# Up-projections of a two-block transformer in fp32r: the three 256-column products of a weight tile become one 512-column and one 256-column product, wide ones first

## The chip, the cores and the metric

One NeuronCore of a Trainium2 chip runs the whole program. The time is the device time of one execution in microseconds; a lower time is better. Three executions of the kernel before took 1694.68 to 1696.04 us, median 1695.74 us.

## The reference

A sequence of 256 tokens with 1024 features passes through two blocks, in float32. The first has attention, an MLP, a state-space mixer and a second MLP; the second has, twice over, a SwiGLU, a convolution-plus-differential-attention mixer and another SwiGLU. The change is in the MLPs and the SwiGLUs:

```python
def squared_relu_mlp(x, w1, w2):                 # x (256, 1024), w1 (1024, 4096), w2 (4096, 1024), 2 layers
    return jnp.square(jax.nn.relu(x @ w1)) @ w2

def swiglu(h, w_gate, w_up, w_down):             # h (256, 1024), gate and up (1024, 2816), down (2816, 1024), 4 of them
    return (jax.nn.silu(h @ w_gate) * (h @ w_up)) @ w_down
```

## The kernel before

**Precision.** A float32 operand is split into a high part (cast to fp32r) and a low part (the remainder): `xh`, `xl` for the activations, `wh`, `wl` for the weights, `hh`, `hl` for the hidden values. A product is made of three on TensorE: high by high, high by low and low by high, summed in PSUM.

**Stages.** Ten stages follow each other: attn, mlp, ssm, mlp, ffn1, diff, ffn2, ffn1, diff, ffn2 (`STAGES`, L1783). `xh` and `xl` hold the stage's input transposed, 128 partitions by 8 blocks `k` of 128 features by 256 tokens.

**A dense stage** (`dense`, L994; `mlp`, L1015; `swiglu`, L1037) takes the first 512 hidden columns with `first`, then chunks of 256 columns with `later`: 14 chunks in each of the 2 MLPs ((4096 - 512) / 256) and 9 in each of the 4 SwiGLUs ((2816 - 512) / 256), so 28 and 36 chunks. A chunk makes one up-projection (MLP) or two (SwiGLU: gate, then up), applies the activation, splits the hidden values and, one chunk later (`LAG`, L624), adds its down-projection into four PSUM banks `acc`: 24 products of 512 columns.

**An up-projection** (`up_T`, L808) loads one 1 MB weight tile `st`, casts it to `wh` on ScalarE (2 pieces) and subtracts to `wl` on VectorE (2 pieces; `unit`, L727). For each of two column blocks `j` and eight `k` it makes three products of 256 columns into one PSUM bank `upT`; weights are stationary, activations move:

```python
mm(ps[:, j], wh[:, c], self.xh[:, k], start=k == 0, stop=False)
mm(ps[:, j], wh[:, c], self.xl[:, k], start=False, stop=False)
mm(ps[:, j], wl[:, c], self.xh[:, k], start=False, stop=k == KM - 1)
```

PSUM has 8 banks, of which `acc` holds four during a dense stage. ScalarE's Relu or Silu and a VectorE multiplication read `upT` directly; `split` (L913) makes `hh` (ScalarE) and `hl` (VectorE).

**Order.** All instructions are recorded first and ordered by a list scheduler (`schedule`, L328): on each engine the ready operation with the lowest `prio` (its place in the program plus `BIAS`, L628) goes next, by a cost table (`cost`, L150). The attn, ssm and diff stages use `up`, `up_T` and others, and pass through the same scheduler.

Of the kernel before, what the change touches and what calls it, by code (L numbers as in the profile page):

```python
# [10 lines left out]
F32 = mybir.dt.float32  # L11
F32R = mybir.dt.float32r
AF = mybir.ActivationFunctionType
ALU = mybir.AluOpType
# [113 lines left out]

class Op:
    __slots__ = ("seq", "eng", "call", "args", "kw", "cost", "prio", "preds", "succs", "allocs", "tiles", "table",  # L130
                 "start", "end", "est", "nbytes", "phase", "key")


ENG_OF = {"tensor": "PE", "scalar": "ACT", "vector": "DVE", "gpsimd": "POOL", "sync": "SP"}
# [7 lines left out]
def free(v):  # L142
    return int(np.prod(v.shape[1:]))
# [72 lines left out]
class Recorder:  # L216
# [42 lines left out]
    def record(self, eng, method, args, kw):  # L259
        o = Op()  # L260
        o.seq, o.eng, o.args, o.kw = len(self.ops), ENG_OF[eng], args, kw
        o.call = (eng, method)
        o.table = 0
        if method == "activation":
            f = kw.get("func", args[2] if len(args) > 2 else None)
            o.table = TABLES.get(f, 0)
        if method == "dma_start":
            out, writes, reads = kw["out"], [kw["out"]], [kw["in_"]]
        else:
            out = args[0] if args else kw["out"]  # L270
            writes = [out] + ([kw["accum_out"]] if "accum_out" in kw else [])
            reads = list(args[1:]) + [v for k, v in kw.items() if k not in OUTS]
        o.key = (self.where, getattr(getattr(out, "tile", None), "name", ""), o.eng)
        o.prio = o.seq + self.bias + BIAS.get(o.key, 0)
        writes = [v for v in writes if isinstance(v, View)]
        reads = [v for v in reads if isinstance(v, View)]
        if method == "dma_start":
            big = out if isinstance(out, View) else kw["in_"]
            o.nbytes = 4 * (big.p[1] - big.p[0]) * free(big)
            o.cost = 0.06 if o.eng == "SP" else 1.0  # L280
        else:
            o.nbytes = 0
            o.cost = cost(o.eng, method, args, kw, out, reads)
        o.preds, o.succs, o.allocs, o.tiles = {}, [], [], []
        if self.ahead is not None and self.ops:
            o.preds[self.ops[max(0, min(o.seq - 1, o.seq - self.ahead))]] = 0
        o.phase = None
        for v in reads:
            self.access(o, v, False)
        for v in writes:  # L290
            self.access(o, v, True)
        self.ops.append(o)
        return o
# [34 lines left out]
    def schedule(self):  # L328
# [21 lines left out]
        ready = {e: [] for e in engs}  # L350
        clock = {e: 0.0 for e in engs}
        table = [0]
        dma = [0.0]
        hwdge = [0.0]
        pe = PEClock()
# [74 lines left out]
        while done < total:  # L430
            best = None
            for e in engs:
                r = ready[e]
                if not r:
                    continue
                t0 = clock[e]
                if best is not None and t0 >= best[0]:
                    continue
                cand = [(est_of(o) if o.allocs else o.est, o) for o in r]
                m = min(x for x, _ in cand)  # L440
                t = max(t0, m)
                if t >= INF or (best is not None and t >= best[0]):
                    continue
                c = None
                for x, o in cand:
                    if x <= t + 1e-9:
                        k = o.prio
                        if e == "ACT" and o.table and o.table != table[0]:
                            k += SWITCH
                        if c is None or k < c[0]:  # L450
                            c = (k, o)
                k, o = c
                w = t + o.cost * HOLD
                h = None
                for x, q in cand:
                    if t < x < w and q.prio < o.prio - HOLD_MARGIN:
                        if h is None or q.prio < h[1].prio:
                            h = (x, q)
                if h is not None:
                    t, o = h  # L460
                    if best is not None and t >= best[0]:
                        continue
                best = (t, e, o)
            if best is None:
                self.stuck(npred)
            t, e, o = best
            ready[e].remove(o)
            take(o)
            o.start = t
            c = o.cost  # L470
            if e == "ACT" and o.table and o.table != table[0]:
                c += 1.283
                table[0] = o.table
            end = t + c
            if e == "PE":
                end = pe.run(t, c, columns(o))
            clock[e] = end
            if o.nbytes:
                if e == "SP":
                    hwdge[0] = max(hwdge[0], t + 0.55) + DMA_FIXED  # L480
                    dma[0] = max(dma[0], hwdge[0] + 0.65)
                else:
                    dma[0] = max(dma[0], t + 1.0)
                dma[0] += max(o.nbytes / 2.0 ** 20 * DMA_US, 0.05)
                end = dma[0] + DMA_END
            o.end = end
            order.append(o)
            done += 1
            for t_ in o.tiles:
                left[t_] -= 1  # L490
                last_end[t_] = max(last_end.get(t_, 0.0), end)
                p = t_.pool
                if p.phase >= 0:
                    phase_left[p.phase] -= 1
                    phase_end[p.phase] = max(phase_end[p.phase], end)
                    if phase_left[p.phase] == 0:
                        for q in waiting_phase.pop(p.phase, []):
                            push(q)
                if left[t_] == 0:
                    key = (p, t_.tag)  # L500
                    tagfree[key].append((last_end[t_] + 0.2, t_.slot))
                    held[key].remove(t_)
                    version[key] += 1
            for q in o.succs:
                lat = SAME[e] if q.eng == e else LAT.get((e, q.eng), 0.2)
                if o.nbytes:
                    lat = 0.2
                if q.preds[o]:
                    q.est = max(q.est, end + lat)
                else:  # L510
                    q.est = max(q.est, o.start)
                npred[q] -= 1
                if npred[q] == 0:
                    push(q)
# [34 lines left out]
FP32_MIN = 0.213  # L549
HOLD_MARGIN = 150  # L550
SWITCH = 500
DMA_US = 2.91
DMA_FIXED = 0.5
DMA_END = 0.7
# [2 lines left out]
T = 256  # L557
DM = 1024
KM = DM // 128
# [112 lines left out]
class Net:  # L672
    def __init__(self, tc, ctx, I, out):
# [14 lines left out]
        nc = self.nc  # L688
# [4 lines left out]
        self.neghalf = self.const.tile([128, 16], F32, name="neghalf")  # L693
        nc.gpsimd.memset(self.neghalf, -0.5)
        self.X = self.xp.tile([128, 2, DM], F32, name="X")
        self.xh = self.xp.tile([128, KM, T], F32R, name="xh")
        self.xl = self.xp.tile([128, KM, T], F32R, name="xl")

    def shaped(self, v, shape):

# [107 lines left out]
    def up_T(self, W, col, exact=False):  # L808

        ws = self.unit256(W, col, exact)  # L810
        ps = self.bank([128, 2, T], "upT")
        mm = self.nc.tensor.matmul
        for j in range(2):
            c = slice(j * 128, (j + 1) * 128)
            for k, (wh, wl) in enumerate(ws):
                if exact:
                    mm(ps[:, j], wh[:, c], self.x32[k // 4][:, k % 4], start=k == 0, stop=k == KM - 1)
                    continue
                mm(ps[:, j], wh[:, c], self.xh[:, k], start=k == 0, stop=False)
                mm(ps[:, j], wh[:, c], self.xl[:, k], start=False, stop=False)  # L820
                mm(ps[:, j], wl[:, c], self.xh[:, k], start=False, stop=k == KM - 1)
        return ps

    def bank(self, shape, name):
        return self.psum.tile(shape, F32, tag="ps", name=name)
# [189 lines left out]
    def mlp(self, W1, W2, finish_of):  # L1015
        nc = self.nc
# [8 lines left out]
                self.split_hid(hs, s, t)  # L1025

        def later(tp, c0, h):
            ps = self.up_T(W1, c0)
            r = tp.tile([128, 2, T], F32, tag="r", name="r")
            s = tp.tile([128, 2, T], F32, tag="s", name="s")  # L1030
            nc.scalar.activation(r, ps, AF.Relu)
            nc.vector.tensor_tensor(s, r, ps, op=ALU.mult)
            self.split(h, s)

        self.dense("mlp", DFF, first, later, W2, finish_of)
# [1 line left out]
    def swiglu(self, Wg, Wu, Wd, finish_of):  # L1037
# [11 lines left out]
                self.split_hid(hs, sg[t], t)  # L1049

        def later(tp, c0, h):
            pg = self.up_T(Wg, c0)
            s = tp.tile([128, 2, T], F32, tag="s", bufs=4, name="sg")
            nc.scalar.activation(s, pg, AF.Silu)
            pu = self.up_T(Wu, c0)
            nc.vector.tensor_tensor(s, s, pu, op=ALU.mult)
            self.split(h, s)

        self.dense("ffn", DFF2, first, later, Wd, finish_of)
# [760 lines left out]
```

## Time and profile before

| what | value |
|---|---|
| median of three executions | 1695.74 us (1694.68 to 1696.04) |
| the profiled execution's own time | 1694.3 us |
| its span, first to last instruction | 1692.4 us |
| PE (TensorE products) busy | 1676.7 us, 99% |
| DVE (VectorE) busy | 1123.6 us, 66% |
| ACT (ScalarE) busy | 878.0 us, 52% |
| weight transfers (1 MB each) | 267, landing after 4.8 us (median) |

The profile counts PE as busy from the start of a product to its modelled end, and products overlap in the pipeline: what one product costs in a stream is the distance from its start to the next one's start, not its duration. Names: `upT` is the PSUM bank of an up-projection in a chunk, `acc` a bank of the down-projection, `up` a 512-column projection elsewhere, `tr` a transpose, `wh`/`wl` the split weights, `st` the landed tile, `X` the residual stream. All instructions carry line L539, the place where the scheduler issues them, so the names tell them apart.

### The profile page before, as it was taken

The page shows a single profiled execution, that of the slowest core. Times are in us where ns is not written, and L with a number is a line of the kernel's source. Part 1 is how long each engine was busy: PE and PEld are TensorE (multiplying, and loading weights), DVE is VectorE, ACT ScalarE, POOL GpSimd, SP SyncE. Part 2 cuts the span into 40 slices and gives each one's busy share as a digit, 9 for nine tenths or more (in the row PEclk, how much of TensorE's full clock was granted, in tenths as well). Part 3 has the DMA queues.
Part 4 walks back from the last instruction along what each step waited for, and adds up shares of the span by engine and source line. Part 5 has one row for each costly group of instructions (what it writes and reads, how often), then busy time and mean ns, then how long its engine had stood idle before and what let it go on. Part 6 is the DMA issues. An engine that isn't in the chain of part 4 may idle for free.

```text
span 1692.4 us, 25721 instructions
## 1 busy us (share of the span) xinstructions
PE 1676.7 (99%) x10454; PEld 1476.2 (87%) x10454; DVE 1123.6 (66%) x1702; ACT 878.0 (52%) x1524; POOL 47.2 (3%) x50
## 2 busy tenths in 40 slices
PE   9999999999999999999999999999999999999999
PEld 8888998899988999889998658999899998579998
DVE  7766555899999555585545987554555458976541
ACT  5644444589995444454444366444454343565440
POOL 0000000000000000000000100000000001100000
PEclk9999999999999999999999999999999999999999
DMA  7434455374455555465454137555464532276540
GB/s 295 174 114 185 183 199 202 128 300 161 166 193 187 185 193 206 168 255 205 175 192 157 50 144 279 199 179 207 150 221 178 193 125 94 100 266 231 193 156 26
DMA packets 45703, 305.22 MB, mean 180 GB/s; under 512 B 5072, under 2 KB 5264, under 8 KB 11280
## 3 DMA queue, kind: packets, MB, share of 16 engines
q1 hardware_dynamic: 45584, 303.58, 48.9%
q8 instruction: 82, 1.34, 0.3%
q14 instruction: 37, 0.30, 0.1%
HBM read 302.44 MB, written 1.11 MB: 179 GB/s over the span
## 4 chain that ended last, share of the span: by engine, by line
PE 89%; DVE 7%; ACT 2%; POOL 1%; issue 1%; DMA 0%; SPq 0%; POOLq 0%; DVEq 0%; ACTq 0%
PE upT L539 40%; PE acc L539 30%; PE up L539 13%; PE tr L539 2%; DVE y L539 1%; DVE s L539 1%; DVE wl L539 1%; PE yps L539 1%; PE po L539 1%; DVE X L539 1%; PE sc L539 1%; POOL qr L539 1%; DVE dnmx L539 0%; ACT wh L539 0%; DMA st<-in_pack 0%
## 5 line engine op out<-in xcount | busy, mean ns | idle before, releaser
L539 DVE TENSOR_TENSOR wl<-st,wh 128x1024 fp32r<-128x1024 f32 (+1 forms) x516 | 621.1, 1218 | 410.0 <-PE upT L539 210.0
L539 ACT CAST wh<-st 128x1024 fp32r<-128x1024 f32 (+1 forms) x516 | 528.3, 1047 | 492.4 <-PE acc L539 211.5
L539 PE MATMUL upT<-xh,wh 128*128 128x256 f32 x1968 | 557.2, 283 | 0.0
L539 PE MATMUL upT<-xl,wh 128*128 128x256 f32 x1968 | 557.0, 283 | 0.0
L539 PE MATMUL upT<-xh,wl 128*128 128x256 f32 x1968 | 557.0, 283 | 0.0
L539 PEld LDWEIGHTS upT<-xh,wh 128*128 128x128 f32 x1968 | 375.8, 191 | 7.2 <-issue 0.2
L539 PEld LDWEIGHTS upT<-xl,wh 128*128 128x128 f32 x1968 | 375.7, 191 | 6.1 <-issue 0.3
L539 PEld LDWEIGHTS upT<-xh,wl 128*128 128x128 f32 x1968 | 375.9, 191 | 5.6 <-issue 0.2
L539 PE MATMUL acc<-wh,hh 128*128 128x512 f32 x736 | 292.0, 398 | 0.0
L539 PE MATMUL acc<-wl,hh 128*128 128x512 f32 x736 | 290.5, 395 | 0.0
L539 PE MATMUL acc<-wh,hl 128*128 128x512 f32 x736 | 263.7, 394 | 0.0
L539 PEld LDWEIGHTS acc<-wl,hh 128*128 128x128 f32 x736 | 138.4, 188 | 28.7 <-issue 2.3
L539 PEld LDWEIGHTS acc<-wh,hh 128*128 128x128 f32 x736 | 138.5, 188 | 24.9 <-issue 2.3
L539 PEld LDWEIGHTS acc<-wh,hl 128*128 128x128 f32 x736 | 138.3, 188 | 24.6 <-issue 0.5
L539 PE MATMUL up<-wh,xh 128*128 128x512 f32 (+2 forms) x352 | 135.2, 385 | 2.2 <-ACT xh L539 2.2
L539 PE MATMUL up<-wl,xh 128*128 128x512 f32 (+2 forms) x352 | 135.7, 386 | 0.0
L539 PE MATMUL up<-wh,xl 128*128 128x512 f32 (+2 forms) x352 | 134.7, 385 | 1.0 <-DVE xl L539 1.0
L539 DVE SCALAR_TENSOR_TENSOR y<-ut,dprep,y 128x256 f32<-128x256 f32 x240 | 98.4, 475 | 0.0
L539 PEld LDWEIGHTS up<-wh,xh 128*128 128x128 f32 x352 | 66.1, 188 | 13.7 <-ACT xh L539 2.7
L539 PEld LDWEIGHTS up<-wh,xl 128*128 128x128 f32 x352 | 66.0, 188 | 13.7 <-DVE xl L539 1.6
L539 PEld LDWEIGHTS up<-wl,xh 128*128 128x128 f32 x352 | 66.2, 188 | 11.6
L539 PE MATMUL up<-st,x 128*128 128x512 f32 x128 | 57.3, 595 | 0.0
(209 smaller groups left out, 1310.8 us busy)
## 6 DMA issues: line engine op xcount, KB each, us to landing
st<-in_pack SPq DMA_DIRECT2D x267, 1024.0 KB, 4.8
ar<-a_rows SPq DMA_DIRECT2D x16, 512.0 KB, 9.8
gv<-in_ln_g SPq DMA_DIRECT2D x4, 512.0 KB, 6.8
gv<-in_ln_b SPq DMA_DIRECT2D x4, 512.0 KB, 7.6
gv<-in_ffn_norm SPq DMA_DIRECT2D x4, 512.0 KB, 5.8
rpb_bt<-in_rpb_rows SPq DMA_DIRECT2D x1, 1536.0 KB, 8.1
st<-in_pack SPq DMA_DIRECT2D x2, 640.0 KB, 4.4
X<-in_x SPq DMA_DIRECT2D x4, 256.0 KB, 5.3
```

The source lines that it names most:

```text
L539: fn(*[real(a) for a in o.args], **{k: real(v) for k, v in o.kw.items()})
```

## The change

In the chunks of MLP and SwiGLU, `up_T` is replaced by `up_wide`. `xh` and `xl` become the two halves of one tile `xhl`, `[128, 8, 2, 256]`, so that `xhl[:, k]` is 512 contiguous columns, high then low. For each `j` a bank of its own takes `wh` by `xhl` (512 columns) for all `k`; when the wide products of both `j` are made, `wl` by `xh` (256 columns) is added to the first half of each bank. `gather` sums the two halves: ScalarE copies the second half to SBUF and VectorE adds the first half. In the MLP, Relu and multiplication become one VectorE instruction `max(r, 0) * r`; in the SwiGLU, Silu runs in SBUF. The scheduler gets a bonus of 20 places for products of the width last issued on PE, and 7 ns for a 256-column product after a 512-column one. Other users of `up_T` and `up` keep their products.

```diff
@@ record / schedule
+        o.width = free(out) if o.eng == "PE" else 0
...
+                        if e == "PE" and o.width != width[0]:
+                            k += PE_SWITCH
...
             if e == "PE":
+                if o.width == 256 and width[0] == 512:
+                    c += 0.007
+                width[0] = o.width
                 end = pe.run(t, c, columns(o))
...
+PE_SWITCH = 20
...
-        self.xh = self.xp.tile([128, KM, T], F32R, name="xh")
-        self.xl = self.xp.tile([128, KM, T], F32R, name="xl")
+        self.xhl = self.xp.tile([128, KM, 2, T], F32R, name="xhl")
+        self.xh = self.xhl[:, :, 0]
+        self.xl = self.xhl[:, :, 1]
...
+    def up_wide(self, W, col):
+        ws = self.unit256(W, col)
+        mm = self.nc.tensor.matmul
+        res = [self.bank([128, 2, T], "upW") for _ in range(2)]
+        for j, ps in enumerate(res):
+            for k, (wh, _) in enumerate(ws):
+                mm(ps, wh[:, j * 128:(j + 1) * 128], self.xhl[:, k], start=k == 0, stop=False)
+        for j, ps in enumerate(res):
+            for k, (_, wl) in enumerate(ws):
+                mm(ps[:, 0], wl[:, j * 128:(j + 1) * 128], self.xh[:, k], start=False, stop=k == KM - 1)
+        return res
+
+    def gather(self, dst, banks):
+        for j, ps in enumerate(banks):
+            self.nc.scalar.copy(dst[:, j], ps[:, 1])
+            self.nc.vector.tensor_tensor(dst[:, j], dst[:, j], ps[:, 0], op=ALU.add)
...
@@ mlp, later
-            ps = self.up_T(W1, c0)
...
-            nc.scalar.activation(r, ps, AF.Relu)
-            nc.vector.tensor_tensor(s, r, ps, op=ALU.mult)
+            self.gather(r, self.up_wide(W1, c0))
+            nc.vector.scalar_tensor_tensor(s, r, 0.0, r, op0=ALU.max, op1=ALU.mult)
...
@@ swiglu, later
-            pg = self.up_T(Wg, c0)
             s = tp.tile([128, 2, T], F32, tag="s", bufs=4, name="sg")
-            nc.scalar.activation(s, pg, AF.Silu)
-            pu = self.up_T(Wu, c0)
-            nc.vector.tensor_tensor(s, s, pu, op=ALU.mult)
+            u = tp.tile([128, 2, T], F32, tag="u", bufs=2, name="su")
+            self.gather(s, self.up_wide(Wg, c0))
+            nc.scalar.activation(s, s, AF.Silu)
+            self.gather(u, self.up_wide(Wu, c0))
+            nc.vector.tensor_tensor(s, s, u, op=ALU.mult)
```

What it does to the order, at three places. PE in a chunk of an MLP before: `upT` products of 256 columns (up-projection of the next chunk) and `acc` products of 512 columns (down-projection of the last) stand mixed.

```order
L539 MATMUL upT<-xl,wh 128x256
L539 MATMUL acc_1627<-wh,hh 128x512
L539 MATMUL upT<-xh,wl 128x256
L539 MATMUL acc_1627<-wl,hh 128x512
L539 MATMUL upT<-xh,wh 128x256
L539 MATMUL upT<-xl,wh 128x256
L539 MATMUL acc_1627<-wh,hl 128x512
```

PE in such a chunk with the change: `upW` is a bank of `up_wide`.

```order
L546 MATMUL upW<-xhl,wh 128x512 x4
L546 MATMUL acc_1576<-wh,hl 128x512
L546 MATMUL upW<-xhl,wh 128x512 x7
L546 MATMUL acc_1576<-wh,hh 128x512
L546 MATMUL acc_1576<-wl,hh 128x512
L546 MATMUL acc_1576<-wh,hl 128x512
L546 MATMUL acc_1525<-wh,hh 128x512
L546 MATMUL acc_1525<-wl,hh 128x512
L546 MATMUL acc_1525<-wh,hl 128x512
L546 MATMUL acc_1603<-wh,hh 128x512
L546 MATMUL upW<-xhl,wl 128x256 x16
L546 MATMUL acc_1603<-wl,hh 128x512
```

The 16 narrow products now stand in one run and the wide ones mix with `acc` products of the same width: PE goes from 256 to 512 columns once in the chunk, where it went 18 times. Over the whole program the count falls from 572 to 119. In a SwiGLU chunk the order was 96 narrow, then 24 `acc`; it is 16 wide, 16 narrow, 16 wide, 16 narrow, then 24 `acc`.

VectorE in an MLP chunk, before (`s` is the squared Relu, `hl` the low part of the hidden values, `wl` the weights of chunks ahead):

```order
L539 TENSOR_TENSOR s<-r,upT 128x512
L539 TENSOR_TENSOR wl<-st,wh 128x1024
L539 TENSOR_TENSOR hl<-s,hh 128x512
L539 TENSOR_TENSOR wl<-st,wh 128x1024 x3
```

and with the change:

```order
L546 TENSOR_TENSOR r<-r,upW 128x256
L546 TENSOR_TENSOR wl<-st,wh 128x1024
L546 TENSOR_TENSOR r<-r,upW 128x256
L546 SCALAR_TENSOR_TENSOR s<-r 128x512
L546 TENSOR_TENSOR wl<-st,wh 128x1024
L546 TENSOR_TENSOR hl<-s,hh 128x512
L546 TENSOR_TENSOR wl<-st,wh 128x1024 x2
```

Two additions of 256 columns join the queue, with one weight piece between them; the four `wl` pieces of a chunk stay.

## Rows read from the trace of the kernel before

**Rows 1.** The page: span, busy time of each engine, granted TensorE clock.

```profile
span 1692.4 us, 25721 instructions
PE 1676.7 (99%) x10454; PEld 1476.2 (87%) x10454; DVE 1123.6 (66%) x1702; ACT 878.0 (52%) x1524; POOL 47.2 (3%) x50
...
PEclk9999999999999999999999999999999999999999
```

**Rows 2.** Stretches, a SwiGLU chunk and an MLP chunk: PE, PEld, DVE, ACT, POOL busy, clock, DMA.

```profile
1075.97:1092.95 16.98, 16.98 (x122) 16.02 (x122) 8.55 (x9) 7.30 (x8) 0.00 (x0) 1.00 0.49 184
594.68:605.97 11.29, 11.29 (x74) 10.21 (x72) 6.20 (x7) 5.22 (x7) 0.00 (x0) 1.00 0.51 187
```

**Rows 3.** Chain that ended last, SwiGLU chunks: start us, us, what.

```profile
1070.50 5.47 PE acc L539 x24
1075.97 11.51 PE upT L539 x96
1087.48 5.47 PE acc L539 x24
```

**Rows 4.** Timeline of PE, a run of 512-column products: start, us, what.

```profile
429.13 0.39 PE L539 MATMUL up<-wl,xh 128*128 128x512 f32 x1
...
431.85 0.39 PE L539 MATMUL up<-wl,xh 128*128 128x512 f32 x1
```

**Rows 5.** Chain that ended last, the same product in successive MLP chunks.

```profile
587.11 1.06 PE upT L539 x9
...
598.39 1.06 PE upT L539 x9
```

**Rows 6.** Timeline of PE, widths that alternate.

```profile
427.95 0.40 PE L539 MATMUL up<-wh,xh 128*128 128x512 f32 x1
428.19 0.28 PE L539 MATMUL upT<-xl,wh 128*128 128x256 f32 x1
...
428.67 0.40 PE L539 MATMUL up<-wh,xl 128*128 128x512 f32 x1
```

**Rows 7.** Groups by form: count, busy us, mean ns, idle time before.

```profile
L539 DVE TENSOR_TENSOR hl<-s,hh 128x512 fp32r<-128x512 f32 x28 | 19.3, 688 | 9.6 <-ACT hh L539 9.6
L539 DVE TENSOR_TENSOR s<-r,upT 128x512 f32<-128x512 f32 x28 | 19.2, 684 | 6.5 <-ACT r L539 4.6 <-PE tr L539 0.6
...
L539 ACT CAST hh<-s 128x512 fp32r<-128x512 f32 x28 | 17.4, 622 | 5.9 <-DVE s L539 5.7
...
L539 ACT ACTIVATE r<-upT 128x512 f32<-128x512 f32 x28 | 16.8, 600 | 25.0 <-PE upT L539 25.0
...
L539 DVE TENSOR_TENSOR hl<-tr,hh 128x256 fp32r<-128x256 f32 x32 | 12.5, 418 | 0.7
...
L539 DVE SCALAR_TENSOR_TENSOR X<-X,rs,gv 128x512 f32<-128x512 f32 x16 | 11.3, 745 | 0.0
...
L539 ACT CAST hh<-tr 128x256 fp32r<-128x256 f32 x32 | 10.9, 374 | 8.5 <-PE tr L539 5.0 <-DVE hl L539 3.4
```

**Rows 8.** Waits of PE in the whole program: total us, times, longest.

```profile
PE up L539 <- ACT xh L539: 2.2, 2, 1.8
PE po L539 <- DVE pt L539: 1.9, 3, 0.7
```

**Rows 9.** Chain at the end of the first MLP: last `acc`, first `up` of ssm.

```profile
306.97 3.22 PE acc L539 x14
310.18 6.04 PE up L539 x35
```

**Rows 10.** Groups by form: the two halves of a transposed input.

```profile
L539 DVE TENSOR_TENSOR xl<-tr,xh 128x512 fp32r<-128x512 f32 x40 | 26.2, 682 | 3.8 <-ACT xh L539 3.8
...
L539 ACT CAST xh<-tr 128x512 fp32r<-128x512 f32 x40 | 23.1, 589 | 30.5 <-PE tr L539 29.3
```

**Rows 11.** Groups by form: the casts of weights and what they wait for.

```profile
L539 ACT CAST wh<-st 128x1024 fp32r<-128x1024 f32 x512 | 525.5, 1049 | 486.3 <-PE acc L539 208.1 <-PE upT L539 203.7 <-DMA st<-in_pack 40.7
```

**Rows 12.** DMA issues: count, KB each, median us to landing.

```profile
st<-in_pack SPq DMA_DIRECT2D x267, 1024.0 KB, 4.8
```

More of the change, by code (lines that the diff above doesn't have):

```diff
@@ L130 @@
     __slots__ = ("seq", "eng", "call", "args", "kw", "cost", "prio", "preds", "succs", "allocs", "tiles", "table",
-                 "start", "end", "est", "nbytes", "phase", "key")
+                 "start", "end", "est", "nbytes", "phase", "key", "width")
 ENG_OF = {"tensor": "PE", "scalar": "ACT", "vector": "DVE", "gpsimd": "POOL", "sync": "SP"}
@@ L352, in schedule @@
         table = [0]
+        width = [0]
         dma = [0.0]
```

## Prediction

> **What bounds the kernel now.** I read the page first. PE is busy for 1676.7 of 1692.4 us, which leaves 15.7 us in which it stands, and the granted clock is at its upper level, 2.4 GHz, in every slice [rows 1]. The waits of PE say the same: the longest entry is 2.2 us in the whole program [rows 8]. So time comes off only where PE is given less to do, and is lost where PE is made to wait. Next I cut out one chunk of each kind: PE fills both completely, DVE half of them (8.55 of 16.98 us and 6.20 of 11.29 us), ACT less [rows 2]. The reader is to see that the chunks are pure product streams with room on the other engines.
>
> Then the price of a product in a stream, from start to start. In the SwiGLU chunk 96 narrow products take 11.51 us [rows 3]: 119.9 ns for 256 columns. In a run of 512-column products the starts at 429.13 and 431.85 us are 12 products apart [rows 4]: 226.7 ns. Two narrow ones hence cost 239.8 ns and one wide one 226.7 ns for the same columns: **each product carries 13.1 ns that do not go with its width**. (Check: 96 x 119.9 + 24 x 226.7 ns = 16.95 us; the chunk takes 16.98 [rows 3].)
>
> **The change, term by term.**
>
> *Products.* For each weight tile, column block and k, three narrow products (359.7 ns) become a wide and a narrow one (346.6 ns), 13.1 ns less. There are 28 + 72 = 100 up-projections in chunks (28 in the MLPs, two in each of 36 SwiGLU chunks) with 16 such triples: 1600 x 13.1 ns = **-21.0 us**. The order bears the count out: 4800 `upT` products go, 1600 wide and 1600 narrow `upW` come. They lie on the path that sets the end, since PE does.
>
> *Changes of width.* An MLP chunk takes 598.39 - 587.11 = 11.28 us [rows 5]. Its 48 narrow and 24 wide products make 5.755 + 5.441 = 11.196 us; 0.084 us are left, and the order has 18 changes from 256 to 512 columns and back in it: 4.7 ns for a pair of changes. Where widths alternate, two pairs take 428.67 - 427.95 = 0.72 us [rows 6], 0.36 us each, 13.4 ns above 346.6; this stretch is short and read in steps of 10 ns, so I take 4.7 ns, with 0 and 13.4 as ends. The order falls from 572 such pairs to 119: 453 x 4.7 ns = **-2.1 us** (0 to -6.1).
>
> *Gather.* It adds 200 ScalarE copies and 200 VectorE additions of 256 columns. The nearest rows are a cast from PSUM at 374 ns and a subtraction from PSUM at 418 ns [rows 7]. The 28 Relus (600 ns) go; the MLP's multiplication of 684 ns becomes a `max` and multiply, which I put between 684 and the 745 ns of another three-operand form [rows 7]; Silu and the SwiGLU's multiplication keep their sizes. Together DVE gets about 200 x 418 ns = 84 us and ACT 75 - 17 = 58 us. A SwiGLU chunk then holds 8.55 + 4 x 0.418 = 10.2 us of DVE and 7.30 + 1.50 = 8.8 us of ACT in 16.5 us, an MLP chunk 7.0 and 5.4 in 11.0: no engine but PE becomes the bound. I cost it at **0**. What hides it: the hidden values of a chunk are first read one chunk later. Behind the last narrow product of an MLP chunk stand a copy, an addition, the square, the cast (622) and the subtraction (688) [rows 7], 2.8 us in all against 2.6 before, and the order has their first reader 8 products after the narrow run of the following chunk, over 11 us later. PSUM: an up-projection now takes two of the four banks beside `acc`; a pair is asked for again only after the other pair's up-projection (5.55 us) and the 24 `acc` products (5.45 us), and needs about 1 us after its last product to be emptied. If that cover went, each up-projection would start late and PE would stand.
>
> *Weights.* The same 1 MB tiles, pieces and transfers. At 16.5 instead of 16.98 us the SwiGLU chunk asks for 3% more than 184 GB/s, at 49% of the DMA engines' time [rows 2]; **0**.
>
> *Stage edges.* What is late next is the new input at a stage's start. At the end of the first MLP 14 `acc` products, 3.22 us, stood behind the last transposes of the first half before `up` needed them [rows 9]; in the new order there are 5, worth 5 x 226.7 ns = 1.1 us, and the transposes of the second group. The cast and subtraction they must cover take 589 + 682 ns [rows 10], 1.3 us: barely covered. The first chunks of a stage open two banks per up-projection while `first`'s banks are still in use. I take **+1 us** over all stages, between 0 and +8 (half of the 15.7 us in which PE stands now, once more, since `BIAS` was set for other places in the program).
>
> *Sum:* -21.0 - 2.1 + 1.0 = -22.1 us. The profiled execution took 1694.3 us, 1.4 below the median of 1695.74; on its own time the sum gives 1672.2, on the median **1673.6 us**. The ends of the terms give -27.1 and -13.0: 1668.6 to 1682.7.
>
> **Rivals.**
>
> *The fixed part stays.* No row shows a wide product with sliced weights standing and activations moving; the 226.7 ns are from weights that move. Had it to cost 239.8 ns, as two narrow ones, the first term is 0 and the time 1695.7 - 2.1 + 1 = 1694.6 us, no change. Against it: `acc` and `up` products, with two kinds of operands, have one pace [rows 3, 4]. The Trainium skill, TensorE: Matmul & The Clock Gate, section Back-to-back issue gap, gives a spacing of columns over 2.4 GHz plus 2.5 ns for a warm stream; by that rule a product saved is worth 2.5 ns, 1600 of them 4.0 us, an estimate from that page, and the time would be about 1690.6 us. The trace disagrees: it has 13.1 ns beyond the columns. Chance 0.05.
>
> *The edges give it back.* Six dense stages open and close; if PE stood 1 us longer at each of these 12 edges, in place of 1 in all, the time is 1695.7 - 23.1 + 12 = 1684.6 us. For it: the cover at the MLP's end that shrinks [rows 9]. Against: PE waited only 2.2 us there in all [rows 8], and at the SwiGLUs' ends transposes and `acc` products stand as they did. Chance 0.12.
>
> *Slower: a late weight blocks the gather.* ScalarE's queue is in order, and the copies that free a pair of banks stand among the casts, which wait for transfers of 4.8 us [rows 12]. A pair has 11.0 us. If three transfers came late in a row ahead of a copy, 14.4 + 1.6 us pass and PE stands 5.0 us in that chunk. From five such chunks of 36 on the gain is gone; at ten the time is 1695.7 - 22.1 + 50 = 1723.6 us. Against it: of the casts' idle time only 40.7 us are put down to transfers, 412 to PE, which must first free the buffers [rows 11]; weights are early. Chance 0.04.
>
> **How the numbers follow.** The forecast has 0.79. The range, 1668.5 to 1683, is that of its terms and takes in the lighter half of the edges; it leaves out the fixed-part rival (0.05), the blocked gather (0.04) and the rest of the edges, with a little of the forecast, under 0.2. A measurement can tell about 0.2%, 3.4 us. Faster: forecast, edges and a part of the first rival, 0.92; within 0.2%: 0.04; slower: 0.04.
>
> **What would show it.** Right: SwiGLU chunks of 16.5 us and MLP chunks of 11.0 us on the chain; wide `upW` starts 227 ns apart, narrow ones 120; PE's busy time near 1654 us with about as much idle time as now; DVE's busy time near 1208 us and ACT's near 936; no wait of PE for `upW` banks. Wrong: wide starts near 240 ns; a wait of PE for ACT or DVE in front of `upW` or `acc`; idle time of PE above 20 us, gathered at the stage edges; a clock below full in the denser stream.

## The result and the profile after

The changed kernel takes 1676.12 us in the median of 4 runs (1671.69 to 1679.69), the kernel before on the same chip 1695.43 (4 runs): a ratio of 0.9887, 95% interval [0.9875, 0.9898]. The forecast was 1673.6 us in 1668.5 to 1683.0. On a second chip the same two kernels gave 1672.20 and 1694.21 us, 0.9864 [0.9848, 0.9881].

The page of the changed kernel: span, busy time of each engine, granted TensorE clock.

```profile
span 1672.2 us, 22864 instructions
PE 1652.7 (99%) x8854; PEld 1391.9 (83%) x8854; DVE 1199.1 (72%) x1902; ACT 924.0 (55%) x1696; POOL 49.1 (3%) x50
...
PEclk9999999999999999999999999999999999999999
```

A digit stands for 42 us, so this row hides a fall of the clock of a few us; the mean over this execution is 0.999. Against [rows 1] PE is busy for 24.0 us less and stands for 19.5 us (1672.2 - 1652.7) where it stood for 15.7. DVE gets 75.5 us more work and ACT 46, which costs nothing as long as PE waits for neither in a chunk. PEld is busy 84 us less: 1600 loads of weights are gone with the 1600 products (10454 and 8854).

The chain that ended last, in the SwiGLU chunks:

```profile
1082.27 11.11 PE upW L546 x64
1093.38 5.47 PE acc L546 x24
1098.84 11.11 PE upW L546 x64
```

64 products in 11.11 us stand where 96 took 11.51 [rows 3], and `acc` is the same 5.47 us. A chunk takes 1098.84 - 1082.27 = 16.57 us (before 16.98, forecast 16.5).

Timeline of PE, the narrow runs of two successive MLP chunks and then three runs of a SwiGLU chunk (start, duration, what):

```profile
608.28 2.08 PE L546 MATMUL upW<-xhl,wl 128*128 128x256 f32 x16
619.29 2.08 PE L546 MATMUL upW<-xhl,wl 128*128 128x256 f32 x16
...
1085.73 2.08 PE L546 MATMUL upW<-xhl,wl 128*128 128x256 f32 x16
1087.65 3.82 PE L546 MATMUL upW<-xhl,wh 128*128 128x512 f32 x16
1091.30 2.08 PE L546 MATMUL upW<-xhl,wl 128*128 128x256 f32 x16
```

16 narrow products take 1087.65 - 1085.73 = 1.92 us, 120 ns each; 16 wide ones 3.65 us, 228 ns each. An MLP chunk takes 619.29 - 608.28 = 11.01 us (11.28 before [rows 5], forecast 11.0).

Stretches as in [rows 2], one SwiGLU and one MLP chunk: PE, PEld, DVE, ACT, POOL busy, clock, DMA.

```profile
1082.27:1098.84 16.57, 16.57 (x90) 14.34 (x89) 10.15 (x13) 8.55 (x12) 0.00 (x0) 1.00 0.53 192
604.70:615.71 11.01, 11.01 (x58) 9.43 (x57) 6.77 (x8) 5.16 (x7) 0.00 (x0) 1.00 0.52 193
```

PE fills both chunks still. DVE holds 10.15 us of the SwiGLU chunk, as worked out (10.2).

Groups by form: the products, and the gather with what it waits for.

```profile
L546 PE MATMUL upW<-xhl,wh 128*128 128x512 f32 x1600 | 403.4, 390 | 0.0
...
L546 PE MATMUL upW<-xhl,wl 128*128 128x256 f32 x1600 | 208.5, 283 | 0.0
...
L546 DVE TENSOR_TENSOR r<-r,upW 128x256 f32<-128x256 f32 x56 | 23.2, 418 | 55.3 <-ACT r L546 55.3
...
L546 ACT COPY r<-upW 128x256 f32<-128x256 f32 x56 | 20.7, 370 | 56.0 <-PE upW L546 56.0
...
L546 DVE SCALAR_TENSOR_TENSOR s<-r 128x512 f32<-128x512 f32 x28 | 19.3, 691 | 0.8
```

The `upW` products have no idle time ahead of them: in 3200 products PE never waits for a bank. The engines of the gather wait for PE, not PE for them. The prices are those read off related forms [rows 7]: 418 ns for the addition, 370 for the copy (374 taken), 691 for `max` and multiply (684 to 745 taken).

PE's own waits, the longest entries, in us, times, longest:

```profile
PE up L546 <- ACT xhl L546: 3.2, 1, 3.2
PE tr L546 <- DVE X L546: 2.0, 2, 1.1
...
PE tr L546 <- ACT s L546: 1.8, 3, 1.3
```

None of the three lies in a chunk: the first is in the first 16 us, the second at the opening of the second MLP, the third in the attention stage. The kernel before has neither of the last two among its waits, of which [rows 8] shows the longest.

The timeline places the second one, at the end of the state-space stage:

```profile
535.35 1.29 PE L546 MATMUL tr<-ident,X 128*128 128x128 f32 x8 [0.86 <-DVE X L546]
...
541.42 0.63 PE L546 MATMUL tr<-ident,X 128*128 128x128 f32 x4 [1.13 <-DVE X L546]
```

One thing was not forecast. Two of the first four runs took 1671.69 and 1673.98 us, the other two 1678.25 and 1679.69, at mean granted clocks of 0.995 and 0.997 where the first two have 0.999. The experiments below deal with that too.

### The profile page after: what moved, and what is told of

Same layout as the page of the kernel before. It is cut to its first block, busy times and chain, and to the rows that moved or that the text cites. A ratio compares the mean times of both kernels' runs of the same rounds, so it can differ in the third digit from the quotient of the medians.

```text
span 1672.2 us, 22864 instructions
## 1 busy us (share of the span) xinstructions
PE 1652.7 (99%) x8854; PEld 1391.9 (83%) x8854; DVE 1199.1 (72%) x1902; ACT 924.0 (55%) x1696; POOL 49.1 (3%) x50
## 4 chain that ended last, share of the span: by engine, by line
PE 48%; DVE 7%; POOL 1%; issue 0%; ACT 0%; POOLq 0%; DVEq 0%
PE upW L546 24%; PE acc L546 17%; PE up L546 6%; DVE y L546 4%; PE tr L546 1%; POOL qr L546 1%; DVE s L546 1%; DVE dnmx L546 1%; DVE wl L546 0%; DVE X L546 0%; POOL rs L546 0%; DVE hn L546 0%; PE upT L546 0%; DVE nat L546 0%; PE ms L546 0%
## 5 line engine op out<-in xcount | busy, mean ns | idle before, releaser
L546 DVE TENSOR_TENSOR wl<-st,wh 128x1024 fp32r<-128x1024 f32 x516 | 623.0, 1219 | 220.4 <-PE upW L546 113.0
L546 PE MATMUL upW<-xhl,wh 128*128 128x512 f32 x1600 | 403.4, 390 | 0.0
L546 PEld LDWEIGHTS upW<-xhl,wh 128*128 128x128 f32 x1600 | 297.5, 188 | 59.7
L546 PE MATMUL up<-wh,xhl 128*128 128x512 f32 (+2 forms) x704 | 221.0, 386 | 3.6 <-ACT xhl L546 3.2
L546 PEld LDWEIGHTS upW<-xhl,wl 128*128 128x128 f32 x1600 | 205.3, 191 | 7.8
L546 PE MATMUL upW<-xhl,wl 128*128 128x256 f32 x1600 | 208.5, 283 | 0.0
L546 PEld LDWEIGHTS up<-wh,xhl 128*128 128x128 f32 x704 | 130.6, 190 | 28.7 <-ACT xhl L546 3.7
L546 PE MATMUL upT<-xhl,wh 128*128 128x256 f32 x736 | 138.9, 287 | 0.0
L546 PE MATMUL up<-wl,xhl 128*128 128x512 f32 (+2 forms) x352 | 136.1, 387 | 0.0
L546 PEld LDWEIGHTS upT<-xhl,wh 128*128 128x128 f32 x736 | 116.0, 191 | 1.6 <-issue 0.5
```

What stands on the lines that cost most here:

```text
L546: fn(*[real(a) for a in o.args], **{k: real(v) for k, v in o.kw.items()})
```

## The experiments

Each is compared with the kernel before on the same chip. The first four ran on one chip; the longer gather, the first run without the bonus in attention, the filler and the smaller biases on another; the second run without the bonus in attention and the run without the scheduler's lines on a third.

**The changed kernel again.** No edit.

> The changed kernel once more, to see what spreads its times over 8 us where those of before lie within 1.4. Theory: the stretches in which the granted clock stands at 0.5 differ from run to run; runs with a mean clock of 1.000 then lie near 1670 us and each 0.001 less costs about 0.8 us (half speed for 3.4 us). Rival: waits that differ from run to run at a full clock; then times from 1671 to 1680 come with a mean clock of 1.000 too.

Measured: 1672.20 us (1671.39 to 1673.37), ratio 0.9864 [0.9848, 0.9881]. The profiled execution, with the clock at its upper level throughout:

```profile
span 1669.6 us, 22864 instructions
PE 1651.8 (99%) x8854; PEld 1391.5 (83%) x8854; DVE 1198.1 (72%) x1902; ACT 923.9 (55%) x1696; POOL 48.9 (3%) x50
```

None of these four runs has a clock under 0.999, so they do not decide between the theory and its rival; the later runs do. This execution, called undisturbed below, is the cleanest account. The span is 22.8 us shorter than before's [rows 1]: 24.9 us less of busy PE, 2.1 us more of standing PE (17.8 against 15.7).

Part of the busy time goes outside the chunks. These stretches run from the first to the last of the 96 `acc` products of the attention stage, in the kernel before and in this execution:

```profile
71.63:126.15 54.52, 54.52 (x283) 42.80 (x282) 36.97 (x61) 26.12 (x58) 0.90 (x1) 1.00 0.27 92
```

```profile
72.80:124.41 51.61, 51.33 (x276) 41.16 (x276) 35.30 (x59) 26.16 (x58) 0.92 (x1) 1.00 0.26 92
```

The bonus has moved products here, and the stretch takes 2.9 us less; it starts 1.2 us later, so that it ends 1.7 us earlier. With the bonus off in attention alone (below) it takes 54.55 us again.

**Narrow product right behind its wide one.** The same products in another order; the scheduler's bonus off as well.

```diff
-            for k, (wh, _) in enumerate(ws):
+            for k, (wh, wl) in enumerate(ws):
                 mm(ps, wh[:, j * 128:(j + 1) * 128], self.xhl[:, k], start=k == 0, stop=False)
-        for j, ps in enumerate(res):
-            for k, (_, wl) in enumerate(ws):
                 mm(ps[:, 0], wl[:, j * 128:(j + 1) * 128], self.xh[:, k], start=False, stop=k == KM - 1)
-PE_SWITCH = 20
+PE_SWITCH = 0
-                    c += 0.007
+                    c += 0.0
```

> The same wide and narrow products and the same gather, but each narrow product stands right behind its wide one and the scheduler's bonus for equal widths is off: PE goes from 256 to 512 columns 1632 times instead of 119. By the term of the prediction (4.7 ns for a pair of changes) 1513 pairs cost 7.1 us over the changed kernel: about 1683 us; by the alternating stretch (13.4 ns) 20 us, 1696 us. Rival, from the rows of the changed kernel, where a wide product takes 227 ns before a narrow one and a narrow one 120 ns before a wide one: a change of width costs nothing, 1676 us.

Measured: 1687.08 us (1686.05 to 1687.42), ratio 0.9949 [0.9934, 0.9964]. The chain that ended last and, below it, PE's timeline:

```profile
1090.88 11.29 PE upW L546 x64
1102.17 5.50 PE acc L546 x24
1107.67 11.29 PE upW L546 x64
```

```profile
1083.09 0.40 PE L546 MATMUL upW<-xhl,wh 128*128 128x512 f32 x1
1083.34 0.28 PE L546 MATMUL upW<-xhl,wl 128*128 128x256 f32 x1
...
1084.15 0.40 PE L546 MATMUL upW<-xhl,wh 128*128 128x512 f32 x1
```

The same 64 products take 11.29 us where they took 11.11: 0.18 us for about 30 more pairs of changes, 6 ns a pair. By the timeline three pairs take 1.06 us, 353 ns each, against 346.6. So a change of width costs something when it comes every 0.35 us, about 6 to 7 ns a pair in these chunks: between the 4.7 taken and the upper end of 13.4. The chunk is 16.79 us, 0.22 more than 16.57; over 36 SwiGLU chunks this is 8 us, and the MLP chunks (11.14 against 11.01, by the starts of their products) give 4 more; that is 0.13 us for some 15 more pairs, 9 ns a pair. The rest of the 15 us is outside the chunks: about 3 us in the attention stage, where the bonus is off here too.

**The wide product cut in two.** The changed kernel's banks, gather and order, with three narrow products as before.

```diff
-                mm(ps, wh[:, j * 128:(j + 1) * 128], self.xhl[:, k], start=k == 0, stop=False)
+                mm(ps[:, 0], wh[:, j * 128:(j + 1) * 128], self.xh[:, k], start=k == 0, stop=False)
+                mm(ps[:, 1], wh[:, j * 128:(j + 1) * 128], self.xl[:, k], start=False, stop=False)
```

> The changed kernel with each wide product cut into two narrow ones (wh by xh, wh by xl) in the same bank, all else as in the change: banks, order of the runs, gather, scheduler. Theory (13.1 ns for each product beside its width): 1600 more products, 21.0 us more than the changed kernel, about 1696 us. Rival: the gain came from the order, the banks or the shorter wait for weights, and the number of products does not matter: about 1676 us.

Measured: 1695.26 us (1692.77 to 1701.23, 10 runs), ratio 1.0007 [0.9995, 1.0018]. The lowest run is 21.4 us above the lowest of the changed kernel on that chip (1671.39). The chain shows where:

```profile
1100.18 11.51 PE upW L546 x96
```

```profile
607.67 1.12 PE L546 MATMUL upW<-xhl,wl 128*128 128x256 f32 x8
...
618.91 1.12 PE L546 MATMUL upW<-xhl,wl 128*128 128x256 f32 x8
```

96 narrow products are back at the 11.51 us of before [rows 3], in a program whose gather, banks and order are the changed kernel's. Against 64 products in 11.11 us, 32 products fewer are worth 0.40 us, 12.5 ns each; the forecast had 13.1. The second pair of lines is one place in two successive MLP chunks, 618.91 - 607.67 = 11.24 us apart; against 11.01 us, 16 products fewer are worth 0.23 us, 14.4 ns each. Without the wide product the gain is gone.

**The scheduler's lines alone.** The kernel before, with the bonus for equal widths and nothing else.

```diff
+        o.width = free(out) if o.eng == "PE" else 0
+                        if e == "PE" and o.width != width[0]:
+                            k += PE_SWITCH
+                if o.width == 256 and width[0] == 512:
+                    c += 0.007
+                width[0] = o.width
+PE_SWITCH = 20
```

> The kernel before with the scheduler's two lines alone (bonus of 20 places for equal widths, 7 ns for a narrow product behind a wide one): three narrow products, one bank, no gather; changes from 256 to 512 columns fall from 572 to 105. Theory: 467 pairs by 4.7 ns, 2.2 us less than before: about 1693.5 us (1689 to 1696 by the ends 13.4 and 0). Rival: the order is what brought the gain, 1676 us; or the order hurts the stages it was not made for, above 1697 us.

Measured: 1692.81 us (1691.32 to 1697.60, 10 runs), ratio 0.9991 [0.9981, 1.0]. The pairs of changes fall from 572 to 105. The five runs with a clock of 1.0 lie at 1691.32 to 1692.86, those of before on that chip at 1693.77 to 1694.44: about 1.7 us by their medians, the size that the term gives, though the interval reaches 1.0. Three of the ten runs have clocks of 0.996 and 0.997 and take 1695.81 to 1697.60.

The agreement is in part luck. Its page and, in the chain, one place in every second MLP chunk:

```profile
span 1690.6 us, 25742 instructions
PE 1672.8 (99%) x10454; PEld 1475.5 (87%) x10454; DVE 1121.8 (66%) x1702; ACT 877.1 (52%) x1524; POOL 47.8 (3%) x50
```

```profile
595.26 5.15 PE upT L546 x43
...
617.72 5.15 PE upT L546 x43
```

Two MLP chunks take 617.72 - 595.26 = 22.46 us, 11.23 each, where one took 11.29 [rows 2]: about 3 ns for each pair of changes that is gone, or some 1.5 us in 28 chunks. The attention stage gives 1.6 us more, as in the changed kernel (its last `acc` starts at 124.51 us, before at 126.15). Against that PE stands 1690.6 - 1672.8 = 17.8 us, 2.1 more than before and just as long as in the undisturbed execution of the changed kernel, with none of its wide products or gathers.

**A longer gather.** Two more copies in place on each of ScalarE and VectorE for every gathered tile.

```diff
             self.nc.vector.tensor_tensor(dst[:, j], dst[:, j], ps[:, 0], op=ALU.add)
+        for _ in range(2):
+            self.nc.scalar.copy(dst, dst)
+            self.nc.vector.tensor_copy(dst, dst)
```

> The changed kernel with two more in-place copies on ScalarE and two on VectorE behind every gather (100 x 4 instructions of 512 columns, about 0.35 to 0.65 us each), which do nothing to the values: the chain from the last narrow product to the hidden values grows by 2 to 2.4 us per up-projection, and both engines get some 80 to 130 us more. Theory (the gather is covered by a whole chunk): chunks stay at 16.6 and 11.0 us, the time within 3 us of the changed kernel, 1671 to 1677 us. Rival (the gather stands near the path, or VectorE and ScalarE are near their bound): each of 64 chunks loses 0.5 to 2 us, above 1700 us.

Measured: 1677.02 us (1674.07 to 1682.46), ratio 0.99 [0.9878, 0.9922]; two of the four runs have clocks of 0.995 and put the median at the end of the expected range, the other two take 1674.07 and 1674.55. The profiled one is of the former kind. A SwiGLU and an MLP chunk of it, in the columns of before:

```profile
1080.27:1096.84 16.57, 16.57 (x90) 14.34 (x89) 11.56 (x17) 10.81 (x16) 0.00 (x0) 1.00 0.51 188
604.70:615.71 11.01, 11.01 (x57) 9.43 (x57) 7.71 (x11) 6.51 (x10) 0.00 (x0) 1.00 0.57 192
```

```profile
1088.62 11.11 PE upW L546 x64
1099.73 5.47 PE acc L546 x24
1105.20 11.11 PE upW L546 x64
```

ACT's work in a SwiGLU chunk has grown from 8.55 to 10.81 us and DVE's from 10.15 to 11.56. The chunk takes 1105.20 - 1088.62 = 16.58 us, and no wait of PE for `upW` or the chunk's `acc` appears. The gather has room to spare inside the chunks; that it costs nothing there is shown. Its two runs with full clocks are still about 2.5 us above those of the changed kernel. In its profile three waits of PE outside the chunks, for tiles of other stages or a stage's new input, are together 2.4 us longer than in the undisturbed execution (`ptps <- DVE s` 2.9 against 2.0 us, `tr <- DVE hn` 1.5 against 0.3, `tr <- DVE on` 1.5 against 1.2), so at the stages' edges a longer gather seems to cost something.

The same run shows where the mean clock falls. Stretches at the start of the program: this kernel first, then the undisturbed execution of the changed kernel, then, with the bonus off in attention (next experiment), the same stretches:

```profile
36.00:41.00 5.00, 3.45 (x25) 2.60 (x22) 5.00 (x12) 3.12 (x13) 0.00 (x0) 1.00 0.00 0
...
42.00:56.00 14.00, 14.00 (x75) 14.00 (x74) 8.10 (x19) 7.68 (x24) 0.00 (x0) 0.54 0.20 75
```

```profile
36.00:41.00 5.00, 3.57 (x28) 2.81 (x24) 5.00 (x12) 3.11 (x12) 0.00 (x0) 1.00 0.00 0
...
42.00:56.00 14.00, 14.00 (x128) 14.00 (x128) 13.71 (x26) 11.89 (x33) 0.00 (x0) 1.00 0.48 166
```

```profile
36.00:41.00 5.00, 4.87 (x38) 4.23 (x35) 5.00 (x11) 2.58 (x7) 0.00 (x0) 1.00 0.58 210
...
42.00:56.00 14.00, 13.33 (x123) 13.13 (x122) 13.89 (x29) 13.61 (x38) 0.00 (x0) 1.00 0.31 108
```

In the first, PE is busy for 3.45 of the 5 us ahead and then gets a clock of 0.54, nearly all of it at 1.2 GHz: 75 products in 14 us. In the second the bonus is on as well, PE is busy for 3.57 us ahead, and yet the clock stays: 128 products. In the third PE is busy for 4.87 us ahead, and the clock stays. So less work ahead is not enough by itself to bring the fall. The wait in the timeline of PE of the first:

```profile
40.49 0.44 PE L546 MATMUL tr<-ident,s 128*128 128x128 f32 x2 [1.28 <-ACT s L546]
```

With the bonus the 256-column products have been issued earlier, and PE waits 1.28 us for the softmax, in the undisturbed execution too (longest 1.3); without it, they fill that gap. Beside the runs of the same kernel with a clock of 1.0, those with 0.997 or less here and with the order alone lose 1.1 to 1.7 us for each 0.001 of mean clock, not the 0.8 expected of the repeated run.

**The bonus off in the attention stage.** Run twice.

```diff
-                        if e == "PE" and o.width != width[0]:
+                        if e == "PE" and o.width != width[0] and o.key[0] != "attn":
```

> The changed kernel with the bonus for equal widths off in the attention stage alone, so that PE's order there is close to that of before. Theory (the spread of the changed kernel comes from falls of the granted clock in the first 60 us, which the order of the attention stage brings on): no run with a mean clock under 0.999, all runs within 3 us of each other, median 1672 to 1674 us. Rival (the spread has nothing to do with the order there): one run in four or so still shows 0.995 to 0.997 and lies 5 to 8 us above the fastest.

> The changed kernel with the bonus off in the attention stage alone, once more. If the bonus in the attention stage is what lets the granted clock fall in some executions (9 of 32 executions with it have a mean clock of 0.997 or less, none of 12 without it), all runs lie between 1671.5 and 1674.5 us with a mean clock of 0.999 or 1.0. If the 12 were chance, about one run in four is 1676 us or more at 0.997 or less.

Measured: 1672.95 us (1671.87 to 1674.51), ratio 0.9873 [0.9858, 0.9888], and again 1673.89 us (1672.95 to 1674.10), ratio 0.9874 [0.9858, 0.9891]. The medians are near the changed kernel's best runs, and the spread is gone: 8 runs within 2.7 us. Two of them have clocks of 0.998, which the expectation did not allow for; neither is above 1674.1 us. While the clock holds, the bonus in attention is a gain, though: in the undisturbed execution the stage ended 1.7 us earlier, and the changed kernel run again, on another chip, has the lower ratio (0.9864), though the intervals overlap.

**Filler products behind the first transposes.** The last kernel with 12 products of 128 columns (24 in the trace) into a bank that nobody reads, where PE stands for the first activations.

```diff
+            if t == 0:
+                ps = self.bank([128, 512], "fill")
+                for _ in range(FILL):
+                    self.nc.tensor.matmul(ps[:, 0:128], self.ones, self.X[:, 0, 0:128], start=True, stop=True)
+FILL = 12
```

> As the run with the attention stage's old order, and 12 products that nothing reads behind the first eight transposes, where PE stood 3.2 us before the first projection and the granted clock then fell to 0.5 for 3.4 us. Theory: PE stands less, the clock holds, and the runs that lay 1.7 to 3 us above the fastest are gone: all at 1670 to 1672 us. Rival: the fall has another cause, or the filler delays the transposes of the second half: no fewer such runs, or 1 to 2 us more in all of them.

Measured: 1672.25 us (1672.01 to 1673.30), ratio 0.987 [0.9854, 0.9887], all four at a clock of 1.0. The place it fills, first in the changed kernel's first profile, then here:

```profile
8.00:12.00 4.00, 1.39 (x7) 1.19 (x8) 1.91 (x3) 2.98 (x5) 0.00 (x0) 0.92 1.04 410
12.00:16.00 4.00, 4.00 (x26) 4.00 (x25) 3.64 (x5) 2.92 (x4) 0.00 (x0) 0.65 1.01 410
```

```profile
8.00:12.00 4.00, 4.00 (x38) 4.00 (x37) 2.44 (x4) 3.50 (x6) 0.00 (x0) 1.00 1.03 421
12.00:16.00 4.00, 4.00 (x35) 4.00 (x35) 3.64 (x5) 2.55 (x4) 0.00 (x0) 1.00 1.00 406
```

This is a second, smaller fall of the clock, after the wait of 3.2 us, and it is not the change's own: the kernel before has mean clocks of 0.999 in runs that are 1 to 3 us above its others as well, though no profile shows that it falls at this place there. With the filler PE is busy throughout, and the clock stays. Here too standing alone does not bring the fall: the undisturbed execution has PE busy for 2.00 us of the first of these stretches, at a clock of 1.00 in both. This version is near the best runs of the changed kernel, and steadier than the changed kernel; over the last one it gains nothing that the intervals can tell.

**Smaller biases for the MLP's last down-projections.** On top of the filler.

```diff
-    ('mlp', 'acc10', 'PE'): 100,
-    ('mlp', 'acc11', 'PE'): 130,
+    ('mlp', 'acc10', 'PE'): 40,
+    ('mlp', 'acc11', 'PE'): 60,
```

> As the run with the filler, and the MLP's down-projections of the second token half lag less (places 40 and 60 instead of 100 and 130), so that at an MLP's end fewer old products stand ahead of those that close the first half. Theory (the changed kernel loses about 2 us at the ends of the two MLPs, where PE waits 2.0 us for the new input): 1 to 2 us less than the run with the filler, about 1669 us. Rival: the lag also kept PE fed inside the chunks or the stretch behind; same or slower.

Measured: 1675.91 us (1674.93 to 1676.08), ratio 0.9889 [0.9874, 0.9903], 3.7 us slower than with the filler alone. Two of PE's waits that are new or longer (the filler kernel waits 0.2 us for `hn` and not for `xc`):

```profile
PE xnps L546 <- ACT xc L546: 1.1, 1, 1.1
...
PE tr L546 <- DVE hn L546: 1.0, 2, 0.9
```

Of the two settings tried, the biases of before are the better one for the new order too.

**The wide products without the scheduler's lines.** The changed kernel with the bonus and the 7 ns off everywhere.

```diff
-PE_SWITCH = 20
+PE_SWITCH = 0
-                    c += 0.007
+                    c += 0.0
```

> The changed kernel without the scheduler's two lines (bonus 0, 7 ns off); the wide products and the order written in the code stay. The changes from 256 to 512 columns rise from 119 to 287 in the program. By the theory (4.7 to 7 ns for a pair of changes) the chunks lose 168 x 4.7 to 7 ns = 0.8 to 1.2 us, and the scheduler's bonus is worth that plus what it changes at the stage edges: the alternating run had the state-space stage 2.6 us longer, which should show here too if the bonus and not the alternation made it. Time: 1671.6 + 1.0 + 2.6 = 1675.2 us with the edges, 1672.6 without. The rival, that the bonus itself is worth nothing, gives 1671.6. By the theory of the clock no run has a mean granted clock of 0.997 or less, since the attention stage has its old order.

Measured: 1673.62 us (1673.29 to 1674.95), ratio 0.9874 [0.9859, 0.9888]; no run below a clock of 0.999. This lies between the two expectations, 1672.6 and 1675.2. The entry `tr <- DVE X` is gone from PE's waits, and these are among them (2.7 us of the first at the program's first projection):

```profile
PE up L546 <- ACT xhl L546: 3.1, 2, 2.7
...
PE xnps L546 <- ACT xc L546: 1.1, 1, 1.1
```

So that wait for `X` comes with the bonus, and the bonus is worth little on top of the order in the code: between the ratios 0.9864 and 0.9874 lie 1.7 us, with intervals that overlap, and against the first four runs of the changed kernel (0.9887), two of which had the clock fall, the version without it is not slower. The closest comparison is on the same chip: with the bonus everywhere but in attention 1673.89 us, without it 1673.62, both 0.9874. Outside attention the bonus is worth nothing that can be read, as the rival said.

## Why the prediction was right

*Products, -21.0 us: right.* Cutting the wide product in two gives back 21.4 us and restores the old 11.51 us. A saved product is worth 12.5 ns in a SwiGLU chunk, widths included, and 14.4 in an MLP chunk: 36 x 0.40 + 28 x 0.23 = 20.8 us. Every product here comes with a weight load of its own (as many PEld as PE instructions), so a merge saves a load too; whether the nanoseconds belong to the product or to its load no run separates. The rival "the fixed part stays" is out: wide products with standing weights start 227 to 228 ns apart, as the others do. By the formula of the Trainium skill (TensorE: Matmul & The Clock Gate, section Back-to-back issue gap), columns over 2.4 GHz plus 2.5 ns, which the section gives for the gap of single products and not for a stream with weight loads like this one, 1600 products would have been worth 4.0 us, an estimate from that page. The trace disagrees: in this stream it is 12.5 to 14.4 ns.

*Changes of width, -2.1 us: about right, a little too large, and dependent on the spacing.* With the narrow products kept together an MLP chunk takes 11.23 to 11.24 us in place of 11.29, about 3 ns a pair where 4.7 were taken, some 1.5 us in all; alternation costs 6 to 9 ns a pair. All stand between the ends. The 1.7 us of the order alone are no proof of this term, since the attention stage gave as much.

*Gather, 0: right in the chunks.* There is no wait of PE for `upW`, and a gather that holds ACT for 10.81 us of a SwiGLU chunk in place of 8.55 leaves the chunk at 16.58 us. ACT's forecast of 936 us and DVE's of 1208 came out 924 and 1199; the gather's own instructions had the prices taken, so the difference lies in other groups and was not followed up. The rival of the blocked gather, which began with these copies, has no row for it.

*Weights, 0: right.* The DMA share of a chunk rises from 0.49 and 0.51 [rows 2] to 0.53 and 0.52, and no weight is waited for in a chunk.

*Stage edges, +1 us: within its range, wrong in place and cause.* PE stands 2.1 us longer in the undisturbed execution. The prediction put the danger at the end of the first MLP, where only 5 `acc` products were to cover the cast and subtraction. They do: no wait of PE falls into that place. The new waits are in the attention stage, for the softmax (1.8 us where 0.7 were waited for `pt`), and at the opening of the second MLP, for the last updates of `X` by DVE (2.0 us where 1.0 were waited for `xl`). The bonus makes them: with the scheduler's lines alone PE stands just as long, 2.1 us of it for `X` and 1.6 for the softmax. Of the 2.2 us that the prediction read as waits at the stages' edges [rows 8], 1.8 are the program's first projection. The rival "the edges give it back" asked for 12 us.

*The sum.* Busy PE -24.9, standing PE +2.1, -22.8 us of span in the undisturbed execution, against -23.1, +1.0 and -22.1. The chunks alone give 36 x 0.41 + 28 x 0.27 = 22.3 us of the busy time, 0.8 less than forecast; the other 2.6 us lie outside them, about the size of what the bonus takes from the attention stage, for which the working had no term. That the sum comes out so close is partly luck: this gain and the longer standing nearly cancel.

*What failed* is one clause of the last part: "a clock below full in the denser stream" was named as a sign against the forecast. The clock did fall in some executions, and not in the dense stream but in the attention stage, on the one side effect of the change that the working gave no term: the bonus acts on every product of the program, attention's too. Counted over all runs: with the bonus in attention (the changed kernel twice, the cut product, the order alone, the longer gather) 9 of 32 have a mean clock of 0.997 or less; without it (the other five kernels, one of them twice, and all runs of before with a clock on record) none of 24 and, of before, none of 33. On one chip it is 2 of 4 against 0 of 12, on another 5 of 24 against 0 of 4. These runs take 4.5 to 8.5 us more than the fastest of their kernels. That the bonus in attention brings the falls is shown by turning it off there (none of 16 runs, the filler and the smaller biases among them); how it does is not: the same order passes at the full clock in most executions (in the undisturbed one with the same wait of 1.3 us), and what tips it was not settled.

## What to carry to other kernels

Where PE streams products without a gap, count products, not only columns: merge two that share their weights into one wider one, and pay for it on engines with room, if a whole chunk lies between the sum and its reader. Keep equal widths together where the order is free, but look at what such a rule does in every stage that it reaches: in attention it saved 1.7 us while the clock held, and took away work that had kept PE busy, with 4.5 to 8.5 us lost in 9 of 32 runs. Off in that stage alone, the times were steady. Look at the mean granted clock of every run, not only at the profiled one.

## What the runs showed of the hardware that was not expected

The granted clock can stay at its lower level for most of 14 us (0.54 in the stretch from 42 to 56 us) although PE is busy in all of it, when PE was busy for only 3.45 of the 5 us ahead and stood once for 1.28 us; in another execution of the same order of products (3.57 of 5 us, the same wait) it stays at its upper level. A wait of 3.2 us at the start is followed by a shorter fall (0.92, then 0.65 in the next 4 us). A change between products of 512 and 256 columns costs nothing that can be read where it is rare (64 products in two runs of each width: 11.11 us, where 32 x 346.6 ns are 11.09), about 3 ns a pair with 18 pairs in an MLP chunk (11.29 us against 11.23), and 6 to 9 ns where widths alternate.
